# Ada shift and scale: the weight matrix becomes the stationary operand and the activated condition the moving column

## The chip, the cores and the metric

The kernel runs on one NeuronCore of a Trainium2 chip. The metric is device time in microseconds (us) of one execution. Three timed runs of the kernel before gave 1648.79, 1652.58 and 1656.51 us. The engines are named as in the profile: PE is the matrix engine (PEld its weight loads), DVE the vector engine, ACT the scalar engine, POOL the general engine, and SP issues the DMAs. Each engine takes its instructions in order and waits on semaphores of the others.

## The reference, cut to what matters

One layer of an encoder trunk over 2048 tokens of width 1024, in float32. The part that the change touches is the adaLN modulation, which is computed from one condition vector `c` and scales and shifts the normalised input before the big input projection:

```python
c_act = jax.nn.silu(c)                                   # (1, 1024)
mod = c_act @ w_ada[layer] + b_ada[layer]                # (1, 3072)
shift, scale, gate = jnp.split(mod, 3, axis=-1)
h = rmsnorm(x, norm_g) * (1.0 + scale) + shift           # (2048, 1024)
proj = h @ w_in[layer]
```

`proj` feeds a Fourier branch and a gated linear attention branch; both are gated, concatenated, sent through `w_out`, and added to `x` through `gate`. The `gate` third of `mod` is computed elsewhere in the kernel and is not touched.

## The kernel before, in words

The kernel is one long program written in a tile framework. Its scheduler places each instruction in its engine's queue when the instruction is built, so the order on each engine is the scheduler's and need not be that of the code. A tile that is asked for from a pool takes the place of an older tile of the same tag (`bufs` says how many places there are), and its first writer waits until the older one's last reader is done.

The activations `h` are held transposed (features on the 128 partitions, tokens along the free dimension), so `shift` and `scale` are needed as columns: 8 chunks `j` of 128 features each, one column for shift and one for scale per chunk. The start of the program, up to the first large product, runs so (the first half of the tokens, 1024 of them):

- **Loads.** SP issues the small vectors, the tables of the Fourier fold, four slabs `xs` of transposed input (slab `p` holds feature chunks 2p and 2p+1), and per chunk `j` two halves of the reordered `w_ada` (`load_ada`, L918, tiles `ada` of 512 KB, chunks k 0 to 3 in the one and 4 to 7 in the other). The `ada` tiles share the tag `B` and its six places with the split weights of the products that follow, so the loads of chunk j+3 wait for the products of chunk j.
- **Fold and norm.** PE does the fold products (L396). ACT and DVE sum the squares of `xs`, PE reduces them (`ss`, L146), POOL takes the power (L149), and PE spreads the result over the partitions (`rbp`, L165).
- **Ada loop (L929).** For each chunk: eight products with `cact` (the activated `c`) as a one-column stationary operand and 256 columns of the matrix as moving operand give one row of 256 numbers on one partition (`row`, L933). ACT copies the row to `rs` (L935). Two one-row products turn it into two columns `cps` (L938). DVE adds the bias and writes `shift` (L939) and `gs` (L940), which are columns of one tile shown as `vecs`.
- **Scaling, inside the loop after odd j.** DVE multiplies slab p by the norm (`x_scale`, L172, two per slab), ACT applies scale and shift to each of its two chunks (`a_affine`, L181; chunk 2p+kk needs the columns of j = 2p+kk), DVE adds two quarters (L182).
- **Splits, `a_by_operand` (L184).** The products use a seven-product block scheme (as Strassen and Winograd's), each in three passes of a high and a low part. For each of the seven operands n and each slab p, ACT writes the high part `A<n>_hi` and DVE the low part `A<n>_lo` (L48 and L49), with sums on DVE in between (L191 to L194). The weights go the same way (`b_prep`, L207; sums at L229 to L237).
- **First product, `block_tok` (L299) called by `do_v(1, A, 0)` (L949).** For each operand n in the order 1, 6, 2, 7, 5, 4, 3 there are four output tiles `pj` in four PSUM places; each takes twelve products (L316): four slabs p by three passes. `n` = 1 therefore needs `A1_hi` and `A1_lo` of all four slabs before any of its four tiles is complete.

The PSUM pool `pf` of this stage has the tags `ss`, `rbp`, `row` and `cps`, one place each. Much later in the program, after the last input projection (L273), the backward scan (`sc`, `upd`, `ktr`, `ob`, `lg`) is interleaved with the first output products (`po`, L850); that place is named because the prediction comes back to it.

Of the kernel before, what the change touches and what calls it, by code (L numbers as in the profile page):

```python
# [12 lines left out]
F32 = mybir.dt.float32  # L13
# [3 lines left out]
AF = mybir.ActivationFunctionType  # L17
# [4 lines left out]
P = 128  # L22
L = 2048
D = 1024
KT = D // P
# [10 lines left out]
def hybrid_kernel(ctx, tc, i, out):  # L36
    nc = tc.nc
    V, S, G, T = nc.vector, nc.scalar, nc.gpsimd, nc.tensor
# [42 lines left out]
    ones = cp.tile([P, 1], F32, name="ones")  # L81
    vecs = cp.tile([P, 3, KT], F32, name="vecs")
    gs, shift, cact = (vecs[:, n] for n in range(3))
# [16 lines left out]
    def pool(stack, name, **kw):  # L100
        return stack.enter_context(tc.tile_pool(name=name, bufs=1, **kw))
# [7 lines left out]
    pf = pool(xstack, "pf", space=PSUM)  # L109
# [794 lines left out]
    with ExitStack() as st_stack:  # L904
        st = st_stack.enter_context(tc.tile_pool(name="start", bufs=1))
# [12 lines left out]
        def load_ada(j):  # L918
            t = [wp.tile([P, BW], F32, tag="B", name="ada")[:, 0:1024].rearrange("p (k w) -> p k w", k=4) for _ in range(2)]
            for h in range(2):  # L920
                load(t[h], i["w_ada"][j][:, 4 * h:4 * h + 4, :])
            return t
# [5 lines left out]
        A = a_tiles()  # L928
        for j in range(KT):  # L929
            wa = load_ada(j)  # L930
            row = pf.tile([P, 256], F32, tag="row", name="row")
            for k in range(KT):
                T.matmul(row[0:1, :], cact[:, k:k + 1], wa[k // 4][:, k % 4], start=(k == 0), stop=(k == KT - 1))  # L933
            rs = st.tile([P, 256], F32, tag="rs", name="rs", bufs=2)
            S.activation(rs[0:1, :], row[0:1, :], AF.Copy)  # L935
            cps = pf.tile([P, 2], F32, tag="cps", name="cps")
            for w in range(2):
                T.matmul(cps[:, w:w + 1], rs[0:1, w * P:(w + 1) * P], ones[0:1, 0:1], start=True, stop=True)  # L938
            V.tensor_tensor(shift[:, j:j + 1], cps[:, 0:1], bcol[:, j, 0:1], ALU.add)  # L939
            V.scalar_tensor_tensor(gs[:, j:j + 1], cps[:, 1:2], b1[:, j:j + 1], ng[:, j:j + 1], ALU.add, ALU.mult)  # L940
            if j % 2:
                p = j // 2
                x_scale(xs[p], rb)
                a_affine(p, xs[p])
# [38 lines left out]
    pf = pool(xstack, "pf2", space=PSUM)  # L983
# [19 lines left out]
    pf = pool(fstack, "pf3", space=PSUM)  # L1003
# [187 lines left out]
```

## Time and profile before

| | |
|---|---|
| median of three runs | 1652.58 us (1648.79 to 1656.51) |
| profiled execution: its time, its span | 1652.96 us, 1651.2 us |
| PE busy | 1559.2 us, 94% of the span |
| DVE, ACT, POOL busy | 1142.0, 699.6, 53.8 us |
| products that make the rows (L933) | 128 records on PE, first 26.3, last 70.2 us |
| products that make the columns (L938) | 32 records, first 32.9, last 71.4 us |
| copies of the rows on ACT (L935) | 8, from 31.9 to 70.6 us |

The program issues 64 products at L933 and 16 at L938; the profile records each float32 product as two, so there are twice as many records. A row of the timeline gives the start, the length, the engine, the line and operation, the tiles (out<-in), the shapes and the count, and in brackets the idle time of the engine just before with what ended it. A row of the table of stretches gives the busy time of each engine (with its count), the granted clock of PE, the DMA share and GB/s.

### The profile page before, as it was taken

To read this page: it belongs to the slowest core of one execution; us is meant where nothing else is said; L and a number is where in the kernel's file an instruction comes from. 1 tells how busy PE (TensorE), PEld (TensorE's weight loads), DVE (VectorE), ACT (ScalarE), POOL (GpSimd) and SP (SyncE) were. 2 spreads that over 40 slices of the span, in tenths; PEclk is the share of its full clock that TensorE was granted. 3 is DMA by queue.
4 is the path that set the end of the run, shared out by engine and by line. 5 is a ranking of instruction groups with operands and counts; after the bars stand their busy time and mean duration, and the time that the engine had idled before them with its cause. 6 is when DMAs were issued, how large, how long until landed. Compare 5 with 4: busy or idle time off the path is not lost.

```text
span 1651.2 us, 25169 instructions
## 1 busy us (share of the span) xinstructions
PE 1559.2 (94%) x9012; PEld 1349.2 (82%) x9012; DVE 1142.0 (69%) x2328; ACT 699.6 (42%) x1324; POOL 53.8 (3%) x118
## 2 busy tenths in 40 slices
PE   7899999999979899999999999988899999999997
PEld 5599878788879888979998887877778888888886
DVE  3967687897659444877877646668857666776663
ACT  4724243443234101313233316486635544655642
POOL 0000000000000000000000000000000111111110
PEclk9999999999989999999999999989999999999999
DMA  9599799899976789879797779978974445444521
GB/s 347 201 351 396 267 327 362 305 354 350 335 279 257 233 290 365 264 231 329 231 321 224 241 240 327 352 251 270 302 235 147 164 161 175 140 158 162 189 97 66
DMA packets 233870, 425.08 MB, mean 257 GB/s; under 512 B 21009, under 2 KB 123281, under 8 KB 230161
## 3 DMA queue, kind: packets, MB, share of 16 engines
q1 hardware_dynamic: 233600, 423.21, 74.1%
q8 instruction: 71, 1.16, 0.3%
q14 instruction: 55, 0.44, 0.1%
q10 hardware_dynamic: 144, 0.26, 0.0%
HBM read 245.99 MB, written 177.41 MB: 256 GB/s over the span
## 4 chain that ended last, share of the span: by engine, by line
PE 41%; DMA 12%; DVE 10%; ACT 5%; issue 3%; SPq 1%; POOL 0%; DVEq 0%; POOLq 0%; ACTq 0%
PE po L850 18%; PE pj L273 7%; PE pj L316 6%; DMA us<-us_d 3%; DMA wot<-in_w_out 1%; PE mapA L56 1%; DMA us_d<-U 1%; PE on L778 1%; PE upd L56 1%; PE pq L56 1%; PE on L776 1%; DMA B<-btok_d 1%; DMA B<-bcol_d 1%; PE sc L553 1%; DVE A_lo L49 1%
## 5 line engine op out<-in xcount | busy, mean ns | idle before, releaser
L273 PE MATMUL pj<-A_hi,B 128*128 128x512 f32 x1344 | 436.7, 400 | 7.3 <-ACT B L48 3.7
L316 PE MATMUL pj<-B,A_hi 128*128 128x264 f32 (+1 forms) x1792 | 335.7, 288 | 28.6 <-ACT p L323 13.2
L316 PEld LDWEIGHTS pj<-B,A_hi 128*128 128x128 f32 x1792 | 282.7, 192 | 33.7 <-ACT p L323 13.9
L273 PEld LDWEIGHTS pj<-A_hi,B 128*128 128x128 f32 x1344 | 251.7, 189 | 65.7 <-ACT B L48 5.4
L273 PE MATMUL pj<-A_lo,B 128*128 128x512 f32 x672 | 268.2, 399 | 0.0
L316 PE MATMUL pj<-B,A_lo 128*128 128x264 f32 (+1 forms) x896 | 255.1, 287 | 2.3 <-DVE A_lo L49 2.3
L316 PEld LDWEIGHTS pj<-B,A_lo 128*128 128x128 f32 x896 | 172.0, 192 | 2.5 <-DVE A_lo L49 2.5
L273 PEld LDWEIGHTS pj<-A_lo,B 128*128 128x128 f32 x672 | 126.7, 189 | 27.4 <-issue 0.2
L850 PE MATMUL po<-wo_hi,fhi 128*128 128x512 f32 x256 | 105.1, 412 | 4.8 <-ACT fhi L48 3.8
L850 PE MATMUL po<-wo_lo,fhi 128*128 128x512 f32 x256 | 103.0, 402 | 0.0
L850 PE MATMUL po<-wo_hi,ghi 128*128 128x512 f32 x256 | 102.5, 400 | 0.0
L850 PE MATMUL po<-wo_lo,ghi 128*128 128x512 f32 x256 | 102.0, 399 | 0.0
L850 PE MATMUL po<-wo_hi,flo 128*128 128x512 f32 x256 | 95.6, 401 | 0.1
L277 DVE TENSOR_TENSOR u<-u,pj 128x512 f32<-128x512 f32 x96 | 65.4, 682 | 41.6 <-PE pj L273 41.5
L850 PE MATMUL po<-wo_hi,glo 128*128 128x512 f32 x256 | 84.8, 401 | 0.0
L575 DVE SCALAR_TENSOR_TENSOR state<-state,sm,upd 128x256 f32<-128x256 f32 x112 | 48.7, 475 | 43.3 <-PE upd L56 43.0
L48 ACT ACTIVATE B<-raw 128x512 fp32r<-128x512 f32 x72 | 42.8, 625 | 74.4 <-DMA raw<-in_w_in 26.2
L321 DVE TENSOR_TENSOR u<-u,pj 128x264 f32<-128x264 f32 (+1 forms) x96 | 48.6, 512 | 32.5 <-PE pj L316 32.4
L56 PE MATMUL mapA<-PQ,wm 128*128 128x256 f32 x480 | 65.0, 285 | 0.9 <-DVE cm L753 0.9
L553 PE MATMUL sc<-qi,ki 128*128 128x128 f32 x256 | 55.2, 298 | 10.4 <-DVE sb L606 6.6
L56 PEld LDWEIGHTS mapA<-PQ,wm 128*128 128x128 f32 x480 | 61.8, 193 | 2.6 <-ACT PQ L48 1.2
L850 PEld LDWEIGHTS po<-wo_hi,fhi 128*128 128x128 f32 x256 | 48.9, 191 | 16.7 <-ACT fhi L48 4.6
(222 smaller groups left out, 2979.5 us busy)
## 6 DMA issues: line engine op xcount, KB each, us to landing
bcol_d<-B SPq DMA_DIRECT2D x84, 512.0 KB, 5.2
B<-bcol_d SPq DMA_DIRECT2D x84, 512.0 KB, 5.4
btok_d<-B SPq DMA_DIRECT2D x28, 528.0 KB, 8.4
B<-btok_d SPq DMA_DIRECT2D x28, 528.0 KB, 7.0
btok_d<-B SPq DMA_DIRECT2D x28, 512.0 KB, 3.6
B<-btok_d SPq DMA_DIRECT2D x28, 512.0 KB, 6.1
raw<-in_w_in SPq DMA_DIRECT2D x12, 1024.0 KB, 8.9
xs<-in_xT SPq DMA_DIRECT2D x16, 512.0 KB, 10.7
```

The source lines that it names most:

```text
L48: S.activation(hi, src, AF.Copy)
L49: (eng or V).tensor_tensor(lo, src, hi.bitcast(F32), ALU.subtract)
L56: T.matmul(ps, a, b, start=(k == 0), stop=(k == n - 1))
L273: T.matmul(ps[:], B[k][0][:, bq, p, :], A[k][aq][:, p, :], start=(p == 0 and q == 0), stop=(p == 3 and q == 2))
L277: V.tensor_tensor(o, a, ps[:], ALU.add)
L316: T.matmul(ps[:, j, :], A[k][aq][:, p, t * P:(t + 1) * P], B[k][p // 2][:, bq, p % 2, :], start=(p == 0 and q == 0), stop=(p == 3 and q == 2))
L321: V.tensor_tensor(o[:, cut], a[:, cut], ps, ALU.add)
L553: T.matmul(ps[:, h, 0:128], ki[:, c0:c0 + P], qi[:, c0:c0 + P], start=True, stop=True)
L575: V.scalar_tensor_tensor(state[:, h, :], state[:, h, :], dec[:, g:g + 1], up_[:, h, :], ALU.mult, ALU.add)
L776: T.matmul(on[:, h, :], a_[:, h, :], b_[:, hs], start=(k == 0), stop=(sc == 0 and k == 2))
L778: T.matmul(on[:, h, :], pre[hp][2][:, 2 * h + s, 0:128], st_f[hp][:, h, :], start=False, stop=True)
L850: T.matmul(ps[n][:], a, wo[j0 + j][q][:, cs], start=(first and a is yh and q == 0), stop=(last and a is yl))
```

## The change

The matrix becomes the stationary operand: for each chunk `j` and each of its two columns `w`, eight products with a 128x128 block of the matrix as stationary operand and one column of `cact` as moving operand accumulate straight into `cps[:, w]`. The row, its copy on ACT and the two turning products go. The tag `row` no longer takes a PSUM place, and `cps` has two places instead of one. Per chunk PE issues 16 products instead of 8 + 2, ACT one instruction less, DVE the same two.

```diff
         for j in range(KT):
             wa = load_ada(j)
-            row = pf.tile([P, 256], F32, tag="row", name="row")
-            for k in range(KT):
-                T.matmul(row[0:1, :], cact[:, k:k + 1], wa[k // 4][:, k % 4], start=(k == 0), stop=(k == KT - 1))
-            rs = st.tile([P, 256], F32, tag="rs", name="rs", bufs=2)
-            S.activation(rs[0:1, :], row[0:1, :], AF.Copy)
-            cps = pf.tile([P, 2], F32, tag="cps", name="cps")
+            cps = pf.tile([P, 2], F32, tag="cps", name="cps", bufs=2)
             for w in range(2):
-                T.matmul(cps[:, w:w + 1], rs[0:1, w * P:(w + 1) * P], ones[0:1, 0:1], start=True, stop=True)
+                for k in range(KT):
+                    T.matmul(cps[:, w:w + 1], wa[k // 4][:, k % 4, w * P:(w + 1) * P], cact[:, k:k + 1],
+                             start=(k == 0), stop=(k == KT - 1))
             V.tensor_tensor(shift[:, j:j + 1], cps[:, 0:1], bcol[:, j, 0:1], ALU.add)
             V.scalar_tensor_tensor(gs[:, j:j + 1], cps[:, 1:2], b1[:, j:j + 1], ng[:, j:j + 1], ALU.add, ALU.mult)
```

The scheduler places the rest anew. Lines behind L934 are three lower in the changed kernel, so the two DVE lines are L936 and L937 there. On DVE, at the start of the scaling, the columns of j = 0 and then j = 1 (`cps_302`, `cps_322`) stood ahead of the eight multiplications by the norm; `traw` are the raw weights of the first product. Before:

```order
L939 TENSOR_TENSOR vecs_80<-cps_302,bcol_114 128x1
L940 SCALAR_TENSOR_TENSOR vecs_80<-cps_302,b1_116,ng_115 128x1
L229 TENSOR_TENSOR t1_551<-traw_538 128x528
L230 TENSOR_TENSOR traw_538<-traw_538 128x2x264
L939 TENSOR_TENSOR vecs_80<-cps_322,bcol_114 128x1
L940 SCALAR_TENSOR_TENSOR vecs_80<-cps_322,b1_116,ng_115 128x1
L172 TENSOR_TENSOR xs_128<-xs_128,rb_204 128x1024 x2
L172 TENSOR_TENSOR xs_131<-xs_131,rb_204 128x1024 x2
L172 TENSOR_TENSOR xs_134<-xs_134,rb_204 128x1024 x2
L172 TENSOR_TENSOR xs_137<-xs_137,rb_204 128x1024 x2
L229 TENSOR_TENSOR t1_559<-traw_539 128x528
```

Now (`cps_314` is j = 1):

```order
L937 SCALAR_TENSOR_TENSOR vecs_80<-cps_291,b1_116,ng_115 128x1
L229 TENSOR_TENSOR t1_575<-traw_562 128x528
L230 TENSOR_TENSOR traw_562<-traw_562 128x2x264
L229 TENSOR_TENSOR t1_583<-traw_563 128x528
L230 TENSOR_TENSOR traw_563<-traw_563 128x2x264
L172 TENSOR_TENSOR xs_128<-xs_128,rb_204 128x1024 x2
L172 TENSOR_TENSOR xs_131<-xs_131,rb_204 128x1024 x2
L172 TENSOR_TENSOR xs_134<-xs_134,rb_204 128x1024 x2
L172 TENSOR_TENSOR xs_137<-xs_137,rb_204 128x1024 x2
L936 TENSOR_TENSOR vecs_80<-cps_314,bcol_114 128x1
L937 SCALAR_TENSOR_TENSOR vecs_80<-cps_314,b1_116,ng_115 128x1
L49 TENSOR_TENSOR A1_lo_274<-xs_128,A1_hi_273 128x512
```

The columns of j = 1 moved behind the eight multiplications, and the sums on the second raw weight tile moved ahead of them.

On PE, at the end of the Ada loop, part of the first product stood between the last chunks (`B_542` holds the weights of slabs 0 and 1, `B_546` of slabs 2 and 3; `pj_611`, `pj_625`, `pj_642` and `pj_656` are the four tiles of n = 1; `cps_412` turns the row of j = 5, `row_426` is that of j = 6). Before:

```order
L316 MATMUL pj_656<-B_542,A1_hi_273 128x264
L316 MATMUL pj_656<-B_542,A1_lo_274 128x264
L316 MATMUL pj_656<-B_542,A1_hi_273 128x264 x2
L316 MATMUL pj_656<-B_542,A1_lo_274 128x264
L938 MATMUL cps_412<-ones_79,rs_410 128x1 x2
L933 MATMUL row_426<-ada_422,vecs_80 1x256 x4
L933 MATMUL row_426<-ada_423,vecs_80 1x256 x4
L316 MATMUL pj_611<-B_546,A1_hi_273 128x264
L316 MATMUL pj_625<-B_546,A1_hi_273 128x264
L316 MATMUL pj_642<-B_546,A1_hi_273 128x264
```

Now (`ada_440` to `ada_464` are j = 6 and 7):

```order
L934 MATMUL cps_444<-vecs_80,ada_440 128x1 x4
L934 MATMUL cps_444<-vecs_80,ada_441 128x1 x4
L934 MATMUL cps_467<-vecs_80,ada_463 128x1 x4
L934 MATMUL cps_467<-vecs_80,ada_464 128x1 x4
L316 MATMUL pj_635<-B_566,A1_hi_273 128x264 x2
L316 MATMUL pj_635<-B_566,A1_lo_274 128x264
L316 MATMUL pj_635<-B_570,A1_hi_273 128x264 x2
L316 MATMUL pj_635<-B_570,A1_lo_274 128x264
L316 MATMUL pj_649<-B_566,A1_hi_273 128x264 x2
```

All chunks of the Ada loop now stand ahead of the first product, and its tiles are done one after the other, each with all four slabs; before, 36 of its 48 rows for n = 1 (three slabs of all four tiles) stood ahead of the columns of j = 7.

The order is the same again from the end of this block to some 45% of the PE program, and differs from there on. The third place is where the input projections end (L273) and the first output products (L850) begin, on PE. Before, only the scan stood between them, with four `ktr` rows (one for each half unit of the scan); the last of these rows are:

```order
L564 MATMUL ktr_11198<-ident_78,K_11170 128x128 x2
L611 MATMUL ob_11192<-state0_10068,Q_11169 128x256 x2
L493 MATMUL lg_11509<-gt_11502,wab1_10055 128x256 x2
L553 MATMUL sc_11222<-qi_11144,ki_11146 128x128
L554 MATMUL sc_11222<-Q_11169,K_11170 128x64
L553 MATMUL sc_11222<-qi_11144,ki_11146 128x128
L554 MATMUL sc_11222<-Q_11169,K_11170 128x64
L564 MATMUL ktr_11237<-ident_78,K_11170 128x128 x2
L850 MATMUL po_11084<-wo_hi0_10910,fhi_11072 128x512
L850 MATMUL po_11084<-wo_lo0_10911,fhi_11072 128x512
```

Now:

```order
L56 MATMUL upd_11046<-vl_11019,kth_11040 128x256
L56 MATMUL upd_11046<-vh_11018,ktl_11041 128x256
L564 MATMUL ktr_11078<-ident_78,K_11011 128x128 x2
L850 MATMUL po_11108<-wo_hi0_10934,fhi_11096 128x512
L850 MATMUL po_11108<-wo_lo0_10935,fhi_11096 128x512
L850 MATMUL po_11109<-wo_hi0_10934,fhi_11096 128x512
L850 MATMUL po_11109<-wo_lo0_10935,fhi_11096 128x512
L611 MATMUL ob_11072<-state1_10093,Q_11010 128x256 x2
L56 MATMUL upd_11085<-vh_11057,kth_11079 128x256
L56 MATMUL upd_11085<-vl_11058,kth_11079 128x256
L850 MATMUL po_11108<-wo_hi0_10934,flo_11097 128x512
```

The output products begin two half units earlier (24 half units stand ahead of the first one where there were 26), and the scan is mixed with them from there on.

## The prediction

> **What bounds the kernel now.** I read the page first, then a table of stretches over the start, then the timelines of DVE and PE there, and last a stretch further on where the order changes again.
>
> ```profile
> span 1651.2 us, 25169 instructions
> ...
> PE 1559.2 (94%) x9012; PEld 1349.2 (82%) x9012; DVE 1142.0 (69%) x2328; ACT 699.6 (42%) x1324; POOL 53.8 (3%) x118
> ```
>
> PE is busy for 94% of the span, so time is made only where PE waits, runs at a lower clock, or gets less to do. The Ada loop lies in one such place. The stretches give PE, PEld, DVE, ACT and POOL busy, then PE's clock, the DMA share and GB/s:
>
> ```profile
> 40.00:57.00 17.00, 14.70 (x71) 6.18 (x70) 16.14 (x27) 10.39 (x15) 0.00 (x0) 1.00 0.78 277
> 57.00:72.00 15.00, 13.68 (x80) 8.44 (x80) 15.00 (x29) 13.74 (x26) 0.00 (x0) 1.00 0.32 127
> 72.00:76.00 4.00, 1.58 (x10) 1.37 (x11) 4.00 (x9) 2.12 (x4) 0.00 (x0) 1.00 1.01 406
> 76.00:84.00 8.00, 7.09 (x37) 6.79 (x36) 7.97 (x14) 5.19 (x12) 0.00 (x0) 0.58 0.26 104
> 84.00:116.00 32.00, 31.84 (x260) 31.48 (x258) 21.37 (x42) 8.90 (x15) 0.00 (x0) 1.00 0.92 349
> 116.00:128.00 12.00, 9.89 (x73) 9.01 (x73) 10.20 (x16) 5.33 (x12) 0.00 (x0) 1.00 1.04 391
> ```
>
> From 40 to 84 us the full engine is DVE, not PE; from 84 us it is PE. PE waits at 72 to 76 for DVE's split of the last slab, and then runs at clock 0.58 for eight microseconds. So the Ada loop matters through two things: when DVE can start and go through its queue, and what PE has finished of the first product before the last slab arrives.
>
> DVE's timeline:
>
> ```profile
> 38.65 0.16 DVE L939 TENSOR_TENSOR vecs<-cps,bcol 128x1 f32<-128x1 f32 x1 [1.58 <-PE cps L938]
> 38.73 0.21 DVE L940 SCALAR_TENSOR_TENSOR vecs<-cps,b,ng 128x1 f32<-128x1 f32 x1
> 38.85 9.16 DVE L172 TENSOR_TENSOR xs<-xs,rb 128x1024 f32<-128x1024 f32 x8
> ...
> 74.11 0.16 DVE L939 TENSOR_TENSOR vecs<-cps,bcol 128x1 f32<-128x1 f32 x1
> ...
> 74.91 1.29 DVE L49 TENSOR_TENSOR A_lo<-xs,A_hi 128x512 fp32r<-128x512 f32 x2
> 76.11 0.71 DVE L237 TENSOR_TENSOR traw<-traw 128x528 f32<-128x528 f32 x1
> ```
>
> The columns of j = 7 are read only at 74.11, some 2.5 us after their last record on PE: they queue behind splits. A_lo of n = 1, slab 3, starts at 74.91.
>
> PE's timeline:
>
> ```profile
> 27.21 1.95 PE L146 MATMUL ss<-ones,rb 128*128 128x1 f32 x16
> ...
> 43.32 0.60 PE L938 MATMUL cps<-ones,rs 1*128 1x1 f32 x4 [1.16 <-ACT rs L935]
> 43.85 3.61 PE L933 MATMUL row<-ada,vecs 128*1 128x256 f32 x16
> ...
> 75.66 1.00 PE L316 MATMUL pj<-B,A_lo 128*128 128x264 f32 x4 [2.34 <-DVE A_lo L49]
> 77.57 0.81 PE L316 MATMUL pj<-B,A_hi 128*128 128x264 f32 x2 [0.91 <-ACT p L323]
> 78.17 0.42 PE L316 MATMUL pj<-B,A_lo 128*128 128x264 f32 x1
> 78.39 0.64 PE L316 MATMUL pj<-B,A_hi 128*128 128x264 f32 x2
> ...
> 84.03 1.15 PE L316 MATMUL pj<-B,A_hi 128*128 128x264 f32 x8
> 85.01 0.28 PE L316 MATMUL pj<-B,A_lo 128*128 128x264 f32 x1
> ```
>
> One L316 takes 0.22 us at the half clock (78.17 to 78.39); eight take 0.98 at the full one (84.03 to 85.01), 0.122 each. The four slow rows from 75.66 end n = 1 near 76.7.
>
> **PE's own work: nothing.** L146 is the very form that comes in: a 128x128 float32 stationary operand and one moving column, sixteen records in 1.95 us, 0.122 each. A chunk's 16 products are 32 records, 3.9 us. It loses 3.61 (L933) and 0.60 (L938), 4.2 us. ACT's eight copies lie beside a DVE that has no time anyway. That is 0.3 us per chunk to the good, 2.4 in all, on an engine that waits there; I count 0. The bound to the other side is the second rival.
>
> **DVE starts later: +0.6.** The sums on the second raw weight tile now stand ahead of the multiplications by the norm (L172). That tile's row:
>
> ```profile
> L42 SPq DMA_DIRECT2D traw<-in_w_v x2: 333/605/877, 26.4 to 26.7; - x2
> ...
> DMA to landing us min/median/max: 9.2/10.3/11.4
> ```
>
> It lands at 26.7 + 11.4 = 38.1. Two sums of some 0.67 follow, so L172 starts at 39.45, not at 38.85, and ends at 48.55. (The two sums, 1.3 us, then don't follow it; the walk below counts that.)
>
> **A new ring between PE and DVE.** PE's work per chunk is the same to 0.3 us, so the columns of j = 1 are ready about when they were, 38.7, and those of j = 2 at 42.6; but DVE now reads j = 1 behind L172, at 48.6 (before: 38.65). `cps` has two places, so the products of j = 3 wait for that read: 48.9, where L933 of j = 3 started at 43.85. From there each chunk j waits for DVE's read of j - 2, and those reads stand between the splits. I walk DVE's queue in its new order with the spacing of its rows (0.605 us for a split or sum: two from 74.91 to 76.11, with a little for the wider ones; 0.2 for a column pair, 38.65 to 38.85) and ACT's beside it, whose rows are quoted last in this part:
>
> - j = 2 is read at 49.4, j = 3 (PE 48.9 to 52.8) at 55.2, j = 4 (to 56.7) at 63.1, j = 5 (to 60.6) at 67.8. All were done on PE well ahead.
> - j = 6 waits for the read of j = 4: PE 63.4 to 67.3, read at 75.5. j = 7 waits for that of j = 5: PE 68.1 to 72.0.
> - Between the reads of j = 1 and j = 6 stand 37 splits and sums, 22.4 us, with 1.0 for the five pairs and 3.3 of waits for ACT, whose scaling of half a slab (1.24 us, then 0.5 for a high part) can only begin at the read: 48.8 + 26.7 = 75.5.
>
> The same walk in the old order, with PE's times as they were, gives 74.1 for the columns of j = 7 and 74.9 for A_lo of slab 3, as the rows above have it. ACT's rows at the end of the old loop:
>
> ```profile
> 74.43 1.24 ACT L181 ACTIVATE xs<-xs,vecs 128x1024 f32<-128x1024 f32 x1 [1.88 <-DVE vecs L940]
> 75.58 1.66 ACT L48 ACTIVATE A_hi<-xs 128x512 fp32r<-128x512 f32 x3
> ```
>
> **The last slab: +2.8.** ACT scales slab 3 after the read of j = 6, 75.7 to 76.9, writes its high part by 77.5, and DVE starts A_lo at 77.7 instead of 74.91.
>
> **PE then has more left: +4.** Before, 36 of the 48 rows of n = 1 stood ahead of the wait, and 12 behind it. Now tile after tile goes through all four slabs, so nine are done and 39 left: 27 more, 3.3 us at 0.122 and 5.9 at 0.22. The wait from about 73.1 to 77.7 is longer than the one at 72 to 76 that ended in clock 0.58; I take 4, not the 5.9, since n = 6 waits for DVE too (its A_lo of slab 3 comes at 84.8 in the walk) and hides part.
>
> The Trainium skill ("TensorE: Matmul & The Clock Gate", What's actually happening) says that the array falls to half its clock after an idle window of about 3.4 us. Rows 72 to 84 agree. By it the wait from 42.6 to 48.9 would put j = 3 at half speed too, 7.8 us: read at 56.9 instead of 55.2 and all that follows some 1.5 us later; the sum would be 1661.
>
> **Given back: 0.** From 84 us PE is full, so a shift goes through. Only at 116 to 128 us does PE stand idle again, 12.00 - 9.89 = 2.1 us; what waits there are the next weights, whose places PE itself frees. Bounds 0 and -2.1; I take 0.
>
> **The later order: 0, between -8 and +8.** From 45% on the queues are mixed anew, and the one place I can price is where the projections end:
>
> ```profile
> 1098.00:1121.00 23.00, 14.62 (x70) 11.93 (x69) 19.73 (x31) 19.76 (x31) 0.00 (x0) 0.77 0.80 269
> ```
>
> ```profile
> 1106.18 0.53 PE L554 MATMUL sc<-Q,K 128*128 128x64 f32 x2
> 1106.50 0.74 PE L553 MATMUL sc<-qi,ki 128*128 128x128 f32 x2
> ...
> 1119.35 0.33 PE L554 MATMUL sc<-Q,K 128*128 128x64 f32 x2
> 1119.52 0.44 PE L553 MATMUL sc<-qi,ki 128*128 128x128 f32 x2
> ```
>
> PE stands idle there for 23.00 - 14.62 = 8.4 us. The output products now come two half units sooner and could fill it; DVE and ACT are at 86% there, though, so what feeds them may be late as well, and the same can be lost elsewhere. No row tells the sign.
>
> **Sum.** 0.6 and 2.2 are within the 2.8 of the last slab; 2.8 + 4 = +6.8 on the profiled execution's 1652.96 us (its span 1651.2 and 1.8 around it) gives 1659.8. That execution is 0.4 above the median of 1652.58, so the forecast is 1659.
>
> **Rivals.**
>
> 1. *The forecast itself*, PE clock full while it does the Ada products: 1659, from 1653 to 1667 with the later order. Chance 0.47.
> 2. *The one-column products don't keep the clock up.* They move 1 column where L933 moved 256, and PE's clock falls where it does little. L554, whose moving side is short, shows what that costs: two in 0.17 us at 1119.35, two in 0.32 at 1106.18. At 0.24 per record a chunk takes 7.8 us, and PE, not DVE, sets the ring: from 48.9 five chunks of 7.8 end at 87.9; if the clock falls before j = 1, the second spreading of the norm (L165) and with it L172 come some 5 us later and j = 7 ends at 93. The whole of n = 1 follows, 48 rows, about 30 of them slow: 8.8 us, to 96.7 or 101.8, where it was done at 76.7. That is +20 to +25, less 4 that n = 6 then neither waits nor runs slowly: 1669 to 1674. For it: the shape. Against it: no row of a long run of this form; L146 is 1.95 us at clock 1.00. Chance 0.25. The Trainium skill (same page, Part 4: PE-mode transpose) notes that transposes don't count as PE being busy in the same way; no run here shows whether this form does.
> 3. *Faster by the late order.* The output products fill the 8.4 us at 1098 to 1121, and the start loses less than 6.8 because the wait at 116 gives 2.1 back: 1659 - 8 - 2 = 1649. With the clock at 0.77 there some 5 of the 23 us are lost to speed as well, and with those back it is 1644. It decides if PE's idle time in that place falls under 2 us. For it: the order, in which PE has other work to hand. Against it: DVE and ACT at 86%. Chance 0.19.
> 4. *The change doesn't reach the path*: DVE's queue is as long as before and catches up by the time PE is full, so the shift is under 2 us: 1653 to 1655. For it: DVE is at 21.37 of 32 after 84 us. Against it: PE is full there and can't catch up. Chance 0.09.
>
> **How the numbers follow.** About 0.5%, 8.3 us, is what a measurement of this kernel can tell from no change: faster is under 1644, slower over 1661. Rival 1 ends about two fifths slower (0.20) and three fifths within (0.27); rival 2 slower (0.25); rival 3 half faster (0.10), half within (0.09); rival 4 within (0.09). Slower 0.45, same 0.45, faster 0.10. Range 1648 to 1675: the upper end is that of rival 2, the lower cuts off half of rival 3; rival 1's own is 1653 to 1667.
>
> **What would show it.** Right: L172 starts near 39.5; the columns of j = 1 are read behind it; PE idles some six microseconds before j = 3; A_lo of slab 3 starts between 77 and 80; the tiles of n = 1 end between 83 and 87 where they ended at 76.7; PE stays shifted by about 7 us up to 450. Wrong: PE's records of L934 spaced by 0.24 (rival 2), PE full again by 84 (rival 4), or the gap at the end of L273 closed (rival 3).

## The result and the profile after

The changed kernel takes 1680.51 us (median of 4 runs, 1678.74 to 1682.33) against 1652.15 for the kernel before beside it: ratio 1.0155, 95% interval 1.0130 to 1.0181. By that ratio it is about 26 us slower; the two medians lie 28.4 us apart. The profiled execution has a span of 1678.0 us.

The page of the changed kernel, its span, the busy times, and the clock of PE in 40 slices of 42 us each:

```profile
span 1678.0 us, 25382 instructions
...
PE 1579.7 (94%) x9108; PEld 1387.1 (83%) x9108; DVE 1141.3 (68%) x2328; ACT 706.2 (42%) x1322; POOL 57.7 (3%) x118
...
PEclk8599999999989999999999999979999999999999
```

PE is busy 20.5 us longer than before (1579.7 for 1559.2), and in the clock one slice stands out, the second, from 42 to 84 us, at 0.5. The 7 is the slice from 1091 to 1133 us, where the projections end.

The table of stretches over the start of the changed kernel (busy PE, PEld, DVE, ACT, POOL, then PE's clock, DMA share and GB/s):

```profile
28.00:32.00 4.00, 4.00 (x33) 4.00 (x34) 0.45 (x3) 1.19 (x2) 1.65 (x1) 0.89 1.08 350
32.00:48.00 16.00, 16.00 (x78) 16.00 (x76) 10.22 (x11) 4.23 (x6) 0.00 (x0) 0.50 0.77 307
48.00:52.00 4.00, 2.24 (x12) 2.15 (x11) 3.46 (x8) 1.98 (x2) 0.00 (x0) 0.50 0.72 235
52.00:84.00 32.00, 32.00 (x152) 32.00 (x152) 25.49 (x47) 20.35 (x31) 0.00 (x0) 0.50 0.37 135
84.00:88.00 4.00, 4.00 (x19) 4.00 (x20) 3.87 (x9) 3.60 (x6) 0.00 (x0) 0.50 0.67 270
88.00:92.00 4.00, 4.00 (x31) 4.00 (x30) 3.40 (x6) 2.20 (x6) 0.00 (x0) 0.86 0.00 0
...
116.00:128.00 12.00, 11.84 (x99) 11.63 (x97) 5.67 (x13) 2.95 (x5) 0.00 (x0) 1.00 1.03 417
```

PE and its weight loads are busy for all of 32 to 48 and of 52 to 84 us, and the clock is at 0.50 throughout. DVE, which was the full engine from 40 to 84 us, is now at 25.49 of 32.

PE's timeline there:

```profile
27.96 3.67 PE L934 MATMUL cps<-vecs,ada 128*128 128x1 f32 x30
31.49 2.06 PE L165 MATMUL rbp<-ident,ms 128*128 128x128 f32 x8
33.34 4.69 PE L934 MATMUL cps<-vecs,ada 128*128 128x1 f32 x22
37.89 2.05 PE L165 MATMUL rbp<-ident,ms 128*128 128x128 f32 x8
39.74 8.53 PE L934 MATMUL cps<-vecs,ada 128*128 128x1 f32 x40
50.04 34.30 PE L934 MATMUL cps<-vecs,ada 128*128 128x1 f32 x160 [1.76 <-DVE vecs L937]
84.19 0.79 PE L316 MATMUL pj<-B,A_hi 128*128 128x264 f32 x2
```

The first thirty one-column records take 0.122 us each, the last 160 take 0.214. The last chunk ends at 84.2 instead of the 72.0 of the forecast. The wait at the ring is 1.76 us, not six: the slow products fill it.

DVE's timeline, four rows that the prediction's walk had at 39.45 (L172), 55.2 (the columns of j = 3) and 77.7 (A_lo of slab 3), and the read of j = 7:

```profile
40.61 9.17 DVE L172 TENSOR_TENSOR xs<-xs,rb 128x1024 f32<-128x1024 f32 x8 [1.26 <-ACT rb L167]
...
57.06 0.16 DVE L936 TENSOR_TENSOR vecs<-cps,bcol 128x1 f32<-128x1 f32 x1 [0.63 <-PE cps L934]
...
81.05 0.69 DVE L49 TENSOR_TENSOR A_lo<-xs,A_hi 128x512 fp32r<-128x512 f32 x1 [0.75 <-ACT A_hi L48]
...
84.71 0.15 DVE L936 TENSOR_TENSOR vecs<-cps,bcol 128x1 f32<-128x1 f32 x1
```

DVE now waits for PE (j = 3) where PE was to wait for DVE. A_lo of slab 3 comes at 81.05, and the columns of j = 7 at 84.71.

To see where the loss is made, the same record (the n-th of its line) is looked up in both traces; its start in us:

| record | before | after | shift |
|---|---|---|---|
| L316, 48th (end of n = 1) | 76.2 | 92.2 | +16.0 |
| L316, 96th | 85.7 | 98.0 | +12.3 |
| L273, 937th | 431.4 | 441.7 | +10.2 |
| L273, last | 1098.1 | 1108.7 | +10.5 |
| L850, first | 1120.1 | 1130.3 | +10.2 |
| L850, 595th | 1329.3 | 1347.1 | +17.8 |
| L850, 757th | 1388.0 | 1414.9 | +26.9 |
| L850, last | 1641.3 | 1668.1 | +26.7 |

Ten microseconds are lost at the start, and some sixteen behind 1120 us: eight of them by 1200, and nine between 1330 and 1390. (2.4 of these come back by 1401, since the n-th record of a reordered stretch need not be the same product; 2 more are lost by 1470.) PE's timeline of the changed kernel there, only the rows with a wait, and its clock:

```profile
1375.71 0.39 PE L56 MATMUL upd<-vh,ktl 128*128 128x256 f32 x1 [0.72 <-DVE ktl L49]
...
1378.18 0.49 PE L553 MATMUL sc<-qi,ki 128*128 128x128 f32 x2 [1.29 <-DVE ki L522]
...
1380.33 1.09 PE L816 MATMUL otr<-ident,o 128*128 128x128 f32 x4 [1.66 <-DVE sr L818]
...
1382.95 0.79 PE L850 MATMUL po<-wo_hi,ghi 128*128 128x512 f32 x1 [1.54 <-ACT ghi L48]
```

```profile
1370.00:1380.00 10.00, 6.66 (x40) 5.31 (x38) 7.61 (x17) 5.23 (x15) 1.31 (x2) 0.97 0.39 129
1380.00:1390.00 10.00, 8.13 (x29) 6.38 (x30) 8.32 (x16) 6.24 (x10) 1.68 (x3) 0.69 0.35 127
```

Four waits in a row, 5.2 us, and a mean clock of 0.69 behind them. All the waits of PE in the matching stretch of the kernel before, 1290 to 1405 us:

```profile
PE po L850 <- DVE xr L856: 0.8, 1, 0.8
PE otr L816 <- DVE sr L818: 0.6, 1, 0.6
PE sc L554 <- DVE K L543: 0.4, 1, 0.4
```

In these rows PE waits each time for DVE or ACT, which work on what PE has just made: the scan's steps form a chain through three engines. In the trace of before, 17 records of L850 (1352.75 to 1356.75 us) stand between the `ktr` and the `upd` of this step and cover that chain; now it is 3 (1373.71 to 1374.50).

### The profile page after: what moved, and what is told of

Same layout as the page of the kernel before. It is cut to its first block, busy times and chain, and to the rows that moved or that the text cites. A ratio compares the mean times of both kernels' runs of the same rounds, so it can differ in the third digit from the quotient of the medians.

```text
span 1678.0 us, 25382 instructions
## 1 busy us (share of the span) xinstructions
PE 1579.7 (94%) x9108; PEld 1387.1 (83%) x9108; DVE 1141.3 (68%) x2328; ACT 706.2 (42%) x1322; POOL 57.7 (3%) x118
## 4 chain that ended last, share of the span: by engine, by line
PE 50%; DMA 9%; DVE 5%; ACT 4%; issue 2%; SPq 1%; POOL 0%; DVEq 0%; POOLq 0%; ACTq 0%
PE po L850 19%; PE pj L316 12%; PE pj L273 7%; PE mapA L56 3%; DMA us<-us_d 3%; PE pq L56 2%; DMA B<-btok_d 2%; PE upd L56 1%; PE on L778 1%; DMA wot<-in_w_out 1%; PE on L776 1%; PE sc L553 1%; DMA us_d<-U 1%; PE sc L554 1%; DMA B<-bcol_d 1%
## 5 line engine op out<-in xcount | busy, mean ns | idle before, releaser
L273 PE MATMUL pj<-A_hi,B 128*128 128x512 f32 x1344 | 436.7, 400 | 7.5 <-ACT B L48 3.7
L316 PE MATMUL pj<-B,A_hi 128*128 128x264 f32 (+1 forms) x1792 | 336.4, 288 | 22.9 <-ACT p L323 11.2
L273 PEld LDWEIGHTS pj<-A_hi,B 128*128 128x128 f32 x1344 | 250.9, 189 | 67.0 <-ACT B L48 5.4
L316 PEld LDWEIGHTS pj<-B,A_hi 128*128 128x128 f32 x1792 | 285.1, 194 | 25.5 <-ACT p L323 11.6
L273 PE MATMUL pj<-A_lo,B 128*128 128x512 f32 x672 | 267.1, 398 | 0.0
L316 PE MATMUL pj<-B,A_lo 128*128 128x264 f32 (+1 forms) x896 | 256.8, 287 | 0.0
L316 PEld LDWEIGHTS pj<-B,A_lo 128*128 128x128 f32 x896 | 173.3, 194 | 0.0
L273 PEld LDWEIGHTS pj<-A_lo,B 128*128 128x128 f32 x672 | 126.7, 189 | 27.7 <-issue 0.2
L850 PE MATMUL po<-wo_hi,fhi 128*128 128x512 f32 x256 | 105.1, 412 | 7.8 <-ACT fhi L48 4.7
L850 PE MATMUL po<-wo_hi,ghi 128*128 128x512 f32 x256 | 103.7, 405 | 1.6 <-ACT ghi L48 1.5
L850 PE MATMUL po<-wo_lo,fhi 128*128 128x512 f32 x256 | 103.7, 405 | 0.0
L850 PE MATMUL po<-wo_lo,ghi 128*128 128x512 f32 x256 | 102.4, 400 | 0.0
L850 PE MATMUL po<-wo_hi,flo 128*128 128x512 f32 x256 | 97.9, 406 | 0.4 <-DVE flo L49 0.4
L850 PE MATMUL po<-wo_hi,glo 128*128 128x512 f32 x256 | 83.7, 399 | 0.0
L850 PEld LDWEIGHTS po<-wo_hi,fhi 128*128 128x128 f32 x256 | 49.4, 193 | 20.0 <-ACT fhi L48 5.7
```

What stands on the lines that cost most here:

```text
L273: T.matmul(ps[:], B[k][0][:, bq, p, :], A[k][aq][:, p, :], start=(p == 0 and q == 0), stop=(p == 3 and q == 2))
L316: T.matmul(ps[:, j, :], A[k][aq][:, p, t * P:(t + 1) * P], B[k][p // 2][:, bq, p % 2, :], start=(p == 0 and q == 0), stop=(p == 3 and q == 2))
L850: T.matmul(ps[n][:], a, wo[j0 + j][q][:, cs], start=(first and a is yh and q == 0), stop=(last and a is yl))
```

## The experiments

Two questions: is the loss at the start the clock, or the new ring and the order on DVE? And is the loss at the end the other order alone? For both it must be possible to change one thing and hold every queue still. The scheduler takes edges that fix an order and add no wait, so a queue can be written out; `LATE` is a list of instructions for each engine:

```diff
+def pin_late(tc):
+    """The last part of every engine's queue in a written order (edges without a wait)."""
...
+            if prev is not None:
+                tc.add_manual_dep(cur, prev.name, mybir.DependencyInfo(mybir.DependencyClass.NoSync, mybir.DependencyReason.DATA), reason="pin")
...
-        hybrid_kernel(tc, aps, o)
+        hybrid_kernel(tc, aps, o); pin_late(tc)
```

Each comparison below is with the kernel before on the same chip (medians 1654 to 1656 us). "Late order" is the order of the last three quarters of each queue.

### Runs 1 and 2: start and late order exchanged

Edit: `LATE` alone. Run 1 is the changed kernel with the late order of before, run 2 the kernel before with the late order of the changed one.

> The changed kernel, with the last three quarters of every engine's queue put into the order that they had before the change (edges that fix the order and add no wait); the first quarter is the changed kernel's own. Theory (the loss is two things: about 10 us at the start, where the one-column products run at half the clock, and about 16 us from the scheduler's other order after 45% of the program): 10 us over the kernel before, 1662 (1659 to 1666), with the shift of +12 at 98 us and +10 from 136 us on, then flat to the end; clock 0.50 from 31 to 88 us. Rival (the later loss follows from the late start, not from the order): some 1678, with the shift growing after 450 us as in the changed kernel.

> The kernel before, with rows and turns, and the last three quarters of every queue in the order of the changed kernel. Theory (two separate losses): shift 0 up to 450 us, then the loss of the later order alone: 1652 + 16 = 1668 (1664 to 1672), made at the stretches where the scan and the output products are mixed (1120 to 1220 us and 1340 to 1440 us). Rival (the later loss follows from the late start): 1652, as before.

Run 1: 1667.34 against 1655.84 us, ratio 1.0071 (1.0051 to 1.0091). The 96th L316 record is shifted by 12.5 us, the 937th of L273 by 9.3, and the first L850 by 10.8; behind that it is nearly flat (12.8 from 1200 to 1390 us). Run 2: 1670.65, ratio 1.0083 (1.0068 to 1.0098), 13.7 us by the ratio and 14.8 by the medians. Its shift is 1.2 us at 431 and 1.2 at the last L273 record, then 9.2 at 1200 and 17.8 at 1388. The excesses of the two ratios add to 1.54%, and the change as a whole measured 1.55%. So there are two losses, nearly independent, and the second needs no Ada product of the new form.

### Run 3: 64 equal columns

```diff
-            cps = pf.tile([P, 2], F32, tag="cps", name="cps", bufs=2)
+            cps = pf.tile([P, 2, 64], F32, tag="cps", name="cps", bufs=2)
...
-                    T.matmul(cps[:, w:w + 1], wa[k // 4][:, k % 4, w * P:(w + 1) * P], cact[:, k:k + 1],
+                    T.matmul(cps[:, w], wa[k // 4][:, k % 4, w * P:(w + 1) * P], cact[:, k:k + 1].to_broadcast([P, 64]),
```

> As the first run, start order of the changed kernel and later order of before, but each Ada product moves the same column 64 times (64 equal columns, of which one is read) over the same 128x128 weights. Theory (PE's clock falls because one moving column keeps the array idle, though PE and its weight loads are busy all the time): clock 1.00 from 26 to 72 us, 0.12 us per record, the chunk's products in 3.9 us, and then what the walk of the prediction gave: A_lo of slab 3 near 78, n = 1 done at 84 to 87, total 1652 + 3 to 7 = 1655 to 1659. Rival (the weight loads, the two places of cps and the order on DVE set the pace, not the clock): 0.21 us per record as with one column, n = 1 done at 92, total 1662 as the first run.

1664.63 us, ratio 1.0052 (1.0035 to 1.0068): neither. The stretches of run 3:

```profile
28.00:40.00 12.00, 12.00 (x110) 12.00 (x109) 3.74 (x8) 3.37 (x6) 1.65 (x1) 1.00 1.04 384
40.00:44.00 4.00, 0.94 (x9) 0.80 (x8) 4.00 (x5) 1.87 (x2) 0.00 (x0) 0.80 1.05 415
44.00:48.00 4.00, 0.00 (x0) 0.00 (x0) 4.00 (x5) 0.00 (x0) 0.00 (x0) 0.50 0.72 265
...
52.00:84.00 32.00, 32.00 (x151) 32.00 (x151) 25.67 (x49) 19.89 (x31) 0.00 (x0) 0.50 0.38 136
84.00:88.00 4.00, 4.00 (x25) 4.00 (x24) 3.96 (x7) 3.88 (x7) 0.00 (x0) 0.65 0.63 253
```

Up to 40 us theory holds: clock 1.00 and 110 records in 12 us, where one column had fallen to 0.50. Then PE waits at the ring as the prediction had it (7.98 us, until DVE has read j = 1 at 48.5), the clock falls, and 64 columns don't bring it back: 160 records at 0.21 us for 34 us. That need not mean that regaining the clock takes more than keeping it. At half the clock the records themselves come more slowly, so the same 64 columns are some 300 per microsecond (64 in 0.214) where they were 540 (64 in 0.119); one limit between the two would do the same.

### Run 4: the one-column form in the old order

Edit: `LATE` holds every queue of the kernel before from first to last; the sixteen products of a chunk stand where the last product of its row stood.

> The one-column form with every queue in the order of the kernel before, from first to last: the sixteen products of a chunk stand where the eight of its row stood, the turns and the copies on ACT are left out, and DVE reads the columns where it did. Theory (clock): 64 of the products still stand in one block, so the clock falls to 0.50 at some 31 us as before and stays there until the block's end; a chunk takes 6.8 us, the columns of j = 7 come some 8 to 10 us late, and only 12 instead of 39 rows of n = 1 are left behind them: 1652 + 6 to 10 = 1658 to 1662. Rival (DVE's order and the two places of cps make the loss at the start): 1652 to 1654.

1669.84 us, ratio 1.0087 (1.0068 to 1.0105): 14 us lost, above what either expected. So the loss needs neither the new order nor the ring. At the 96th L316 record it is 12.7 us, as in run 1 with the changed order (12.5); why it was not the 6 to 10 expected is open. Its PE timeline:

```profile
41.92 27.31 PE L934 MATMUL cps<-vecs,ada 128*128 128x1 f32 x128
...
74.29 0.42 PE L316 MATMUL pj<-B,A_lo 128*128 128x264 f32 x1
74.51 3.79 PE L934 MATMUL cps<-vecs,ada 128*128 128x1 f32 x32
78.17 1.36 PE L316 MATMUL pj<-B,A_hi 128*128 128x264 f32 x5
...
80.86 4.02 PE L934 MATMUL cps<-vecs,ada 128*128 128x1 f32 x32
```

The 128 records from 41.92 take 0.213 us each. But the 32 at 74.51, behind five microseconds of L316, take 0.118, and the five L316 behind those are slow again (five from 78.17 to 79.33, 0.23 us each, against 0.122). The clock answers to what was moved in the few microseconds before. (Run 8 below has the same order on every engine and 128 columns; it shows what of the 14 us is the columns.)

### Runs 5, 6 and 7: 128 columns, four places, 16 columns

Run 5 has 128 equal columns instead of 64, run 7 has 16. Run 6 has 64 columns and four PSUM places:

```diff
-            cps = pf.tile([P, 2, 64], F32, tag="cps", name="cps", bufs=2)
+            cps = pf.tile([P, 512], F32, tag=("cps0", "cps1", "ss", "rbp")[j % 4], name="cps")[:, 0:128].rearrange("p (w n) -> p w n", w=2)
```

> As the run with 64 columns, same order on every engine, but 128 equal columns per product. The run with 64 columns kept the clock at 1.00 as long as it was up, but after the 8 us wait at the ring (41 to 49 us) its products stayed at 0.50 for 34 us. Theory (the clock follows how much of the time columns are moved, and a rise needs more of it than staying up): 128 columns, 0.14 us per record at full clock and twice that at half, bring the clock back within 4 to 8 us of 48.9; then the ring sets the pace as the prediction's walk had it, j = 7 ends at 72 to 75 instead of 83, n = 1 at 84 to 87, total 4 to 8 us over before: 1660 to 1664 on this chip. Rival (weight loads hold the clock down whatever is moved, or the clock needs a different engine state): half clock to the end of the loop, 0.26 us per record, j = 7 ends at 90, total 14 to 18 over.

> As the run with 64 columns, same order on every engine, but the columns go round four PSUM places instead of two, so that no chunk waits for DVE's read of the one two before. Theory (clock and ring together make the loss at the start; without the wait the clock never falls in the loop): clock 1.00 and 0.12 us per record from 26 to 62 us, all chunks done by 62, then PE waits for the last slab, which DVE's queue gives at 76 to 79; n = 1 done at 84 to 87, total 5 to 8 us over before. This is the prediction's own sum without a clock loss in the loop. Rival (the clock doesn't matter for the end, since PE waits for DVE's splits anyway): the same 9 over as with two places.

> As the run with 64 columns, same order, but 16 equal columns per product. One look at where the clock falls. Theory (the clock follows the share of time in which columns are moved): 16 columns are a quarter of 64, too few to hold it: 0.50 from some 31 us as with one column, total as with one column, 10 to 12 over before. Rival (any more than one column holds it): 1.00 until 41 us as with 64.

Run 5: 1659.45 against 1654.66 us, ratio 1.0029 (1.0011 to 1.0048), as theory had it. Its stretches:

```profile
40.00:44.00 4.00, 1.05 (x10) 0.86 (x8) 4.00 (x5) 1.87 (x2) 0.00 (x0) 1.00 1.04 416
44.00:48.00 4.00, 0.00 (x0) 0.00 (x0) 4.00 (x4) 0.00 (x0) 0.00 (x0) 0.76 0.68 265
48.00:52.00 4.00, 2.30 (x11) 2.33 (x12) 3.45 (x9) 2.37 (x2) 0.00 (x0) 0.50 0.03 8
52.00:56.00 4.00, 4.00 (x33) 4.00 (x33) 3.56 (x7) 1.68 (x4) 0.00 (x0) 0.88 0.15 49
56.00:76.00 20.00, 14.91 (x129) 14.38 (x127) 18.37 (x36) 14.94 (x24) 0.00 (x0) 1.00 0.42 152
```

The clock falls in the wait at 41 to 49.7 us; 0.88 over 52 to 56 means that it was back at about 53. At the half clock 128 columns come every 0.213 us, 600 per microsecond, against the 300 of run 3. The last chunk ends at 72.75, where the forecast had 72.0.

Run 6: 1658.59, ratio 1.0031 (1.0012 to 1.0050). The total is what theory said, but the clock isn't: PE waited 0.38 and 1.17 us for Ada loads between 40 and 43 us, and the clock fell to 0.50 at 44.9 for the rest of the loop. That cost nothing that shows here (run 5 with the clock up is not faster), since without the ring PE was far enough ahead: it began n = 1 at 73.8 and then waited 1.49 us for slab 3. DVE's timeline in run 6, the reads of j = 1 to 6 and the A_lo of slab 3:

```profile
48.38 0.15 DVE L936 TENSOR_TENSOR vecs<-cps,bcol 128x1 f32<-128x1 f32 x1
...
49.17 0.15 DVE L936 TENSOR_TENSOR vecs<-cps,bcol 128x1 f32<-128x1 f32 x1
...
55.02 0.15 DVE L936 TENSOR_TENSOR vecs<-cps,bcol 128x1 f32<-128x1 f32 x1
...
62.88 0.15 DVE L936 TENSOR_TENSOR vecs<-cps,bcol 128x1 f32<-128x1 f32 x1
...
67.62 0.15 DVE L936 TENSOR_TENSOR vecs<-cps,bcol 128x1 f32<-128x1 f32 x1
...
75.31 0.15 DVE L936 TENSOR_TENSOR vecs<-cps,bcol 128x1 f32<-128x1 f32 x1
...
77.55 0.69 DVE L49 TENSOR_TENSOR A_lo<-xs,A_hi 128x512 fp32r<-128x512 f32 x1 [0.75 <-ACT A_hi L48]
```

The prediction's walk had 48.6, 49.4, 55.2, 63.1, 67.8, 75.5 and 77.7.

Run 7, a single run: 1663.43 us, clock 0.95 at 28 to 32 us and 0.50 to 88 us, 160 records in 34.28 us. Sixteen columns are as one.

### Run 8: 128 columns in the old order

> 128 equal columns per product, and every queue in the order of the kernel before from first to last; the turns and the copies on ACT left out. A chunk's products take 32 x 0.14 = 4.4 us where rows and turns took 4.2. Theory (form, clock and order are the whole loss): the start as in the kernel before, n = 1 done near 77, total within 2 us of the kernel before. Rival (the form itself costs more than its records show, for instance because ACT's tables or the loads of the weights come otherwise): 4 us or more over.

1654.92 against 1654.66 us, ratio 1.0010 (0.9994 to 1.0026), and the 48th L316 record starts at 77.2 (before: 76.2). With the columns and the order put right nothing of the 26 us is left: the form with 128 columns costs and gains nothing that can be measured. Run 4 has the very same order on every engine and one column, and is 13 us slower by the ratios (1.0087 and 1.0010): there the number of columns is the only difference.

### Runs 9 and 10: one stretch of the late order

Edit: `LATE` alone. Between 1302 and 1424 us of the kernel before both orders hold the same instructions, so the stretch can be exchanged. It was exchanged on all engines together, so which engine's order makes the loss stays open.

> The kernel before, rows and turns, every queue in its own order except for the stretch that it runs between 1302 and 1424 us, which stands in the changed kernel's order. Theory (the later order loses most in one stretch of the output stage, where PE meets a chain of four waits with too few output products ahead of them): shift 0 to 1300 us, then 8 to 11 us lost before 1390 us, the waits for sr, ghi, ki and ktl at 1.7, 1.5, 1.3 and 0.7 us as in the changed kernel, total +8 to +11. Rival (the loss is spread, or the stretch loses only after what the earlier order left behind): +4 or less.

> The changed kernel in its own order everywhere except for the same stretch, which stands in the order of before. Theory: the changed kernel's +26 less the 8 to 11 of the stretch: +15 to +18. Rival (as above): +22 or more.

Run 9: 1665.35 against 1654.36 us, ratio 1.0067 (1.0049 to 1.0086). PE waits for ghi, sr, ki and ktl for 1.5, 1.4, 1.3 and 0.7 us, so the chain of four waits comes with the order of this stretch. Between the 595th and the 757th L850 record 9.9 us are lost, 2.4 of them come back by 1401, and the shift stays from there at 12.5. So the stretch keeps 7.6 us of its own, a little under the 8 expected; 4.8 were lost ahead of it, 2.7 of them at the seam at some 1280 us. There ACT's queue already has the later order and makes `ghi` ahead of `sh`, while PE still wants `sh` first and waits 1.68 us for it.

Run 10: 1676.57, ratio 1.0136 (1.0113 to 1.0158), which is the rival's number: only some 3 us of the changed kernel's 26 come back. Its trace against the changed kernel's: 6.7 us are won at 1371 to 1400, where the four waits are gone, but 3.5 are lost at the seam, at 1296 to 1300, where PE waits 1.8 us for `ghi`; another 1.4 was behind already at 1250. The seam is that of run 9 the other way round: ACT makes `sh` first (1296.9) and `ghi` only at 1299.1, while PE, still in the changed kernel's order, wants `ghi` first. So a good half of what the stretch would give back is lost because two ACT instructions stand in the other order than PE wants them, and by the two traces the stretch itself is worth 6.7 to 7.6 us.

### Run 11: fillers in the waits

```diff
         a_by_operand(A, xs)
+        fill = pf.tile([P, 128], F32, tag="ss", name="fill")
+        for _ in range(22):
+            T.matmul(fill[:], ident[:], cact[:, 0:1].to_broadcast([P, P]), start=True, stop=True)
```

> 128 equal columns per product and the order of before, as in the eighth run, with 22 more products whose results nobody reads (identity as weights, 128 columns): ten behind the last chunk, where PE waited 2.31 us for A_hi, and twelve behind the next eight records, where it waited 2.31 us for A_lo. Theory (the clock falls in those waits because no columns are moved): the clock stays at 1.00 from 64 to 84 us, the records of n = 1 behind the wait take 0.12 instead of 0.22 us, PE is done with them some 2 to 3 us earlier, and the total is 1 to 3 us under before. Rival (DVE's queue sets the pace there, so a faster PE only waits elsewhere): total as in the eighth run, within 1 us of before.

1655.59 against 1654.36 us, ratio 1.0007 (0.9994 to 1.0020): the rival. Two stretches of run 11:

```profile
72.00:76.00 4.00, 3.93 (x35) 3.74 (x34) 4.00 (x9) 1.84 (x5) 0.00 (x0) 1.00 0.82 326
...
84.00:88.00 4.00, 2.15 (x16) 1.72 (x15) 3.97 (x8) 2.33 (x4) 0.00 (x0) 1.00 0.23 94
```

The clock holds at 1.00 through 72 to 88 us (in run 8 it was 0.62, 0.50 and 0.59 from 72 to 84), and PE simply runs into its next waits for DVE at 84 to 88, 1.85 us in all, with the clock at 0.58 behind them. So the clock of 0.58 at 76 to 84 in the kernel before costs nothing that DVE's queue doesn't cost as well.

### Runs 12 to 15: a third order

Run 12 is the 128-column form with nothing pinned; the scheduler makes yet another order of it. Runs 13 to 15 keep that order up to 660, 870 and 1070 us of before and go on in the order of before.

> The changed kernel with 128 equal columns per product and nothing pinned: the scheduler makes a third order, which differs from both others from 45% of the program on. Theory (the start costs 5 us with this form, and the later order is worth anything between that of before and that of the changed kernel, whatever the edit is for): 5 to 20 over before. Rival (the later order follows from the form, and with the clock restored it is good again): 3 to 6 over before.

> 128 equal columns per product; every queue in the order that the scheduler made for this form (third order) up to what the kernel before runs at 660 us, and in the order of before from there on. The run in the third order throughout was 3 us ahead of before at 150 us, 5 ahead at 660 to 720, 4 ahead at 1095, and 7 behind at the end. Theory (what a stretch of order gains or loses stays with it): 4 to 6 us under before from 660 us to the end, total 1648 to 1651. Rival (a gain made early is lost again where the next transfers or weights have not come, or a seam costs a wait as in the tenth run): within 2 us of before.

> The same with the third order up to 870 us of before. Its run throughout was 2.7 ahead there. Theory: 2 to 4 under before, total 1650 to 1652. Rival: within 2 us of before.

> The same with the third order up to 1070 us of before, so that only the last part, with the scan and the output products, stands in the order of before. Theory (the 11 us between 1095 us and the end are the loss of the last part of the third order alone): 1 to 4 under before, total 1650 to 1653, where the third order throughout gave 1654. Rival (the last part loses whatever its order, because what comes before hands it over differently): as with the third order throughout, or above.

Run 12: 1654.30 against 1654.36 us, ratio 0.9993 (0.9977 to 1.0010); both expectations missed. It is 2.9 us ahead of before at 148 us, 4.1 ahead at the last L273 record, and 7 behind at the end of its profiled execution (1660.25 us, the longest of twelve and 6 above their median). Run 13: 1650.57 against 1655.88, ratio 0.9953 (0.9934 to 0.9972). Run 14: 1655.56, ratio 1.0001 (0.9984 to 1.0018). Run 15: 1650.46, ratio 0.9961 (0.9943 to 0.9980). Run 15 has the order of run 12 up to some 1015 us and ends 3.8 us under it by the medians (the two ran on different chips, and the intervals of their ratios just overlap), so the last part of the third order probably does lose. Run 14 has the order of run 13 but for the stretch from 543 to 861 us, and ends 5 us later; why is open. Its profile doesn't tell, since it is of an execution of 1663.23 us, the longest of twelve, which is already 4.1 us behind at the 937th L273 record, where run 13 in the same order is 0.6 behind.

### Runs 16 and 17: the same best order, one column or 128

Run 16 is the one-column form of the changed kernel with the queues of run 13; run 17 is run 13's kernel again.

> The one-column form of the changed kernel, every queue in exactly the order of the thirteenth run, which with 128 columns ended 5 us ahead of before. Only the number of moved columns differs. Theory (the clock is the start's loss in any order): 0.50 from some 31 us to the end of the loop, 8 to 14 us behind the thirteenth run, total 3 to 9 over before. Rival (in this order DVE sets the pace throughout and the slow products hide beside it): within 3 us of the thirteenth run, still ahead of before.

> The thirteenth run's kernel once more, as the other side of the comparison on the same chip. Expected: 3 to 7 us under before.

Run 16: 1671.75 us against 1656.19, ratio 1.0088 (1.0065 to 1.0110). Run 17: 1649.75, ratio 0.9965 (0.9945 to 0.9985). The number of columns alone, 1 or 128, in one and the same order of every queue, is worth 22 us by the medians and 20 by the ratios; 8 to 14 were expected. The stretch from 36 to 60 us, first of run 16, then of run 17:

```profile
36.00:60.00 24.00, 24.00 (x114) 24.00 (x115) 14.26 (x22) 7.11 (x8) 0.00 (x0) 0.50 0.57 203
```

```profile
36.00:60.00 24.00, 20.21 (x165) 19.86 (x164) 23.43 (x41) 14.75 (x20) 0.00 (x0) 0.93 0.76 281
```

The slow kernel has the busier PE (24.00 of 24) and does 114 records where the other does 165.

## Why the prediction was wrong

The forecast of 1659 fell at two of its steps, "PE's own work: nothing" and "the later order: 0".

- **PE's own work.** The price of 0.122 us was read from L146, sixteen records, 1.95 us long, and those stood behind 16 us of fold products (L396) with 256 columns each, at clock 1.00. The one-column form keeps 0.122 up to some 31 us and then takes 0.214; a chunk is 6.85 us, not 3.9. This was rival 2, at a chance of 0.25. Its mechanism is right (runs 3, 5, 7 and 16), and its price was too high: 0.24 for a record of 0.214, n = 1 done at 96.7 where it was 92.2; the 4 us that it gave back in n = 6 were right (16.0 to 12.3), and 2 more came back behind it. Run 1 gives 11.5 us for the whole start in place of 16 to 21. With 128 columns in that order 4.8 of them remain (run 5), so the slow clock is some 7 us of it; in the other two orders it is 13 (runs 4 and 8) and 20 to 22 (runs 16 and 17).
- **DVE starts later.** 39.45 was right where DVE waits for nothing but the raw weights (39.30 in run 6, 39.46 in run 3; 40.24 in run 5, where they land later). In the changed kernel it is 40.61, since the second spreading of the norm (L165) took 2.05 us at the half clock where run 5 has 1.05, and DVE waited for `rb`.
- **The ring, the last slab.** Where PE is far enough ahead the walk holds to 0.3 us in all seven rows of run 6, A_lo of slab 3 at 77.55 for 77.7. With the ring and the clock up (run 5) the same seven are 0.7 to 0.8 later, as its L172 is. In the changed kernel the ring hardly shows: PE is slower than DVE's reads.
- **PE has more left: +4.** The two steps 2.8 and 4 made 6.8. Run 6 is 4.8 us late at the 96th record, and 2.7 between 128 and 200 us. So the 4 was too much by 2, and the next term by 2 too little.
- **Given back: 0.** About 2 us do come back at 116 to 128 us, the whole of the bound that the prediction named: in the changed kernel PE is busy there for 11.84 of 12 us, before for 9.89. The shift goes from 12.3 to 10.2.
- **The later order: 0, between -8 and +8.** It costs 13.7 us (run 2), outside the bounds too. The one place priced, the end of the projections, gave nothing to either side at its end: the last L273 and the first L850 record are shifted alike, +10.5 and +10.2. The loss lies where the prediction had quoted no row: 7 to 9 us between 1330 and 1400, most of the rest between 1120 and 1200. A place that looks idle was searched for a gain; no place that looks full was searched for a loss.
- **The rivals together.** Rival 2 and the late order were priced each by itself, and the range reached to the larger one. Both happened, and they add.

The prediction's signs worked: the spacing of L934 (it said 0.24 for rival 2) and the end of n = 1 tell the first loss at once. It named no sign for a late loss.

That PE's clock falls with an idle engine was cited from the Trainium skill ("TensorE: Matmul & The Clock Gate", What's actually happening). Run 3 agrees for the wait at 41 to 49 us. The rows at 72 to 84 us, which the prediction also took as agreeing, bear out the fall but not the length: PE's longest wait there is 2.34 us, and the clock fell behind it. And in the changed kernel the clock falls while PE and PEld are busy for all of 28 to 48 us, so the idle share of the profile doesn't tell it; here the measurement decides. The same page's remark on transposes (Part 4: PE-mode transpose), cited beside rival 2, is nearer to what happened, though no transposes were concerned.

## What to carry to other kernels

A matrix-vector product with the matrix as stationary operand is a stream of weight loads that moves almost nothing; in this kernel it ran PE at half clock and slowed everything beside it. If the form is wanted, repeat the column: 128 equal columns took 0.119 us per record (run 5, 32 in 3.81 us), no more than one column at full clock, and brought the clock back after a wait. A price per record must come from a run of records as long as the one that is planned, with the clock of its stretch beside it. And where a scheduler reorders the whole program after a local edit, measure the edit with the rest of the order held still: here that part alone was worth half of the result, and the best mixture of orders (run 13 and 17, 0.9953 and 0.9965) gained 6 to 8 us where the form with 128 columns gained nothing.

## What the runs showed of the hardware

- PE's clock follows the columns moved, not the busy time of the profile. With full weight loads of 128x128 float32 behind each other: 1 and 16 columns fall to 0.50 within 3 to 5 us; 64 keep 1.00 while nothing interrupts them, and so do 128. The old rows, 256 columns over a stationary operand of one column, kept it at 1.00 too (40 to 57 us of the kernel before).
- In all nineteen traces the granted clock is either 1.00 or 0.50; a 0.58 or 0.88 in a table of stretches is the mean of the two.
- After a wait 64 columns stay at 0.50 for 34 us (run 3) and over 28 us (run 6), while 128 are back at 1.00 some 3 us after their first record (run 5). Behind two short waits, 0.38 and 1.17 us, 64 columns lost it. Whether rising takes more than staying up is not shown: in columns per microsecond, 540 kept the clock, 600 brought it back and 300 did not, which one limit would explain as well.
- It lags: 32 one-column records ran at 0.118 us straight behind five microseconds of 264-column records that had run at half clock, and the 264-column records behind them were slow again (run 4).
- The half clock slows a one-column record from 0.122 to 0.214 us (1.75 times) and a 264-column one from 0.122 to 0.22 us.
- Holding the clock up with filler products through two waits worked (1.00 in place of 0.50 to 0.62), and gained nothing, because another engine set the pace (run 11).
